# A squared-ReLU MLP as seven block products instead of eight, in a one-core decoder layer

## The chip, the cores and the metric

The kernel runs on one core of one Trainium2 chip. The metric is the device time of one execution in microseconds (us). A core has TensorE (PE, matrix products into PSUM banks), VectorE (DVE), ScalarE (ACT), GpSimd (POOL) and SyncE (SP). Each of them works through its own queue of instructions in order, and an instruction that waits holds up all that stand behind it. SyncE's queue, and in the changed kernel GpSimd's too, issues the transfers between DRAM and the on-chip memory, which the 16 DMA engines then carry out.

## What is computed

One layer of a decoder trunk, for 1024 tokens of width 1024, with 16 meta tokens ahead of them. Four mixers (pooling, RWKV-7, RG-LRU, mLSTM) read one input projection, their outputs go through one output projection, and a dense MLP follows:

```
h  = layer_norm(x)                                  # embedding norm
mix = concat(pool(u), rwkv7(p), rglru(q), mlstm(r)) # from h @ w_in
h  = layer_norm(ALPHA * h + mix @ w_out)            # ln1, "h1" below
ff = square(relu(h @ mlp_w1)) @ mlp_w2              # 1024 -> 4096 -> 1024
h  = layer_norm(ALPHA * h + ff)                     # ln2, the output
```

Both MLP products are a 1024 x 1024 x 4096 product in float32. The change is in these two.

## The kernel before

Every product of float32 operands is made of three matmuls in a faster float type: each operand is split into a high part (a cast on ScalarE, L120 for weights and L125 for the rest) and a low part (the rest, a subtraction on VectorE, L121 and L126), and high x high, high x low and low x high are summed in PSUM. A product of a 128x128 weight tile with 512 tokens is thus three matmuls of 128x512.

The tokens are in eight tiles of 128, and the mixers work on four blocks of two tiles. `PLAN` is a string of steps that sets the order in which the program is written: `S` input projections, `P`, `I`, `C` the three parts of RWKV (projections and products, the triangular inverse by elimination, the chunk recurrence), `M` mLSTM, `L` RG-LRU, `O` pooling, `W` the output projection with its layer norm, each with its block's number. A scheduler then places the instructions on the engines. The mixers are chains of small operations in which TensorE often has nothing to do, so MLP work of the first 512 tokens is put between them: the steps `F0` to `F6` are seven of the MLP's 16 chunks of 256 hidden units, each 48 matmuls of the first product (`mlp_up`, L1162 to L1164), the activation (ScalarE's relu L1167, VectorE's square L1168) and 48 of the second (`mlp_down`, L1186 to L1188), which adds to an accumulator of its token tile (L1191, L1193). `T` (`mlp_in`) loads the h1 tiles again from DRAM (L1139) and transposes them (L178) into the operand.

Some places matter below. The elimination `I` of block b writes its products to DRAM (`dr<-p`, L693), reads them back (`c<-dr`, L695), runs some 60 small steps on VectorE (L752, L753), and goes through DRAM twice more before the matmuls of L719. The last RWKV step of a block ends in L858; its output goes to DRAM and back (`yd<-ys` L563, `x<-yd` L1104) and is split into the operand `mixh`, `mixl` of the output projection (L1125 to L1127, matmuls of 128x256). The result gets its layer norm (L145, L146, L132, POOL's L133, L164, L169) and is stored as `h1d` (L1113).

When the mixers are done, the "late stage" begins: chunk 7 of the first 512 tokens, then `mlp_in` for the second 512, chunks 8 to 15 for all, and chunks 0 to 7 for the second. The last chunk of a tile is followed by its layer norm (L145, L160, L161) and the store of the output (L162). In all the MLP has 3072 matmuls: 672 between the mixers, 2400 in the late stage.

Of the kernel before, what the change touches and what calls it, by code (L numbers as in the profile page):

```python
# [16 lines left out]
P = 128  # L17
# [14 lines left out]
NC = DFF // 256  # L32
# [11 lines left out]
STEPS = PLAN.split()  # L44
EARLY = sum(t[0] == "F" and t.endswith(".2") for t in STEPS)
# [45 lines left out]
class Trunk:  # L91
# [22 lines left out]
    def load_w(self, src, pool=False):  # L114
        nc = self.nc
        raw = self.wsp.tile([P, 1024], F32, name="wraw", bufs=self.wsb[0])
        nc.sync.dma_start(raw, src)
# [149 lines left out]
    def run(self):  # L267
        tc, nc, a = self.tc, self.nc, self.a
        with ExitStack() as top:
# [5 lines left out]
            self.h1d = [self.drp.tile([P, D], F32, name="h1d%d" % t, bufs=1) for t in range(NT)]  # L275
            self.program(top)

    def program(self, top):
# [9 lines left out]
        self.psp = {"b": psum(top, "psB")}  # L288
# [28 lines left out]
        self.h1t, self.acc = [None] * 2, [None] * NT  # L317
        nf = 0
        for st in STEPS:
# [4 lines left out]
            elif k == "R":  # L324
                R.close()
                self.accp = [pool(M, "acc0", "right", 4), None]
                self.h1p = [pool(M, "h1T0", "right"), None]
                self.mdp, self.mdb = pool(M2, "midA", "right"), 1
            elif k == "T":
                self.mlp_in(0)  # L330
            elif k == "F":
# [801 lines left out]
    def mlp_in(self, g, tag="b"):  # L1133

        self.h1t[g] = [self.h1p[g].tile([P, 8, 512], F32R, name="h1T%s" % x) for x in "hl"]
        for i in range(4):
            t = 4 * g + i
            self.acc[t] = self.accp[g].tile([P, D], F32, name="acc")
            self.nc.sync.dma_start(self.acc[t], self.h1d[t])  # L1139
            self.to_feature(self.acc[t], P, *self.h1t[g], i * P, tag)  # L1140
        self.cnt = getattr(self, "cnt", [0, 0])
# [107 lines left out]
```

## Time and profile before

| | before |
|---|---|
| runs (us) | 1373.75, 1377.15, 1373.67 |
| median | 1373.75 |
| profiled execution | 1368.71 |
| its span, first to last instruction | 1366.9 |
| mean granted TensorE clock | 0.983 |
| moved by DMA | 132.54 MB |

The profile is of the execution that took 1368.71 us; times in it count from the start of its span. A row of the timeline has the start in us, the time in us, the engine, the line, the operation, the tile written and the tiles read, and how many were joined in the row; brackets hold the idle time before it and what ended that. "SPq" is SyncE's queue issuing a transfer, so its time is that of the issue, and the landing comes later. A row of the windows has the stretch, its length, the busy time of PE, PE's weight loads, DVE, ACT and POOL with the number of instructions, the granted clock, the share of the DMA engines and GB/s. A row of the page on DMA ends with the size of one transfer and the median time from issue to landing. The slices cut the span into 40 parts of 34.2 us.

### The profile page before, as it was taken

The numbers are of one execution on the slowest core, as the hardware profiler recorded it, in microseconds if no ns is written. First come the engines' busy times: TensorE is split into PE (matmuls) and PEld (weight loads), VectorE is DVE, ScalarE is ACT, GpSimd is POOL, SyncE is SP. The second block draws the span as 40 slices with busy tenths as digits, with TensorE's granted clock in tenths as the row PEclk, the third lists the DMA queues.
The fourth block names the chain that finished last, engine by engine and source line by source line (L and its number), as shares of the span: only waits on it lengthen the run. The fifth ranks groups of instructions, "written<-read, shape, count | busy, mean of one in ns | idle before, by whom it ended". The sixth has DMA issues, their size and how long they took to land.

```text
span 1366.9 us, 20292 instructions
## 1 busy us (share of the span) xinstructions
PE 1313.2 (96%) x8001; PEld 1110.2 (81%) x8001; DVE 843.2 (62%) x1998; ACT 478.4 (35%) x812; POOL 78.9 (6%) x101
## 2 busy tenths in 40 slices
PE   4999999999999999999999999999999999999997
PEld 3989888988999967777688887888888888788886
DVE  8846657865747668476866875454444544844547
ACT  5435474532376342433332423111211112122320
POOL 3110010000100000010001100000000000100001
PEclk9999999997999999999999999999999999999999
DMA  7422204331443432222323951110111011313311
GB/s 246 173 76 78 74 24 137 104 116 51 136 140 131 166 104 71 70 74 82 112 63 123 321 185 63 47 47 31 62 47 47 31 62 58 112 61 109 123 62 62
DMA packets 60128, 132.54 MB, mean 97 GB/s; under 512 B 22752, under 2 KB 29552, under 8 KB 60032
## 3 DMA queue, kind: packets, MB, share of 16 engines
q1 hardware_dynamic: 60032, 131.23, 29.1%
q8 instruction: 63, 1.03, 0.3%
q14 instruction: 33, 0.27, 0.1%
HBM read 113.38 MB, written 17.83 MB: 96 GB/s over the span
## 4 chain that ended last, share of the span: by engine, by line
PE 50%; DVE 4%; POOL 1%; issue 1%; ACT 1%; DMA 0%; DVEq 0%; ACTq 0%; SPq 0%; POOLq 0%
PE c L1162 7%; PE c L1163 7%; PE c L1164 7%; PE c L1186 6%; PE c L1187 6%; PE c L1188 6%; PE b L1186 1%; PE b L1188 1%; PE b L1187 1%; PE b L1164 1%; PE b L1162 1%; PE b L1126 1%; DVE wlo L121 1%; PE b L1127 1%; PE b L1125 1%; PE b L1163 1%
## 5 line engine op out<-in xcount | busy, mean ns | idle before, releaser
L120 ACT CAST whi<-wraw 128x1024 fp32r<-128x1024 f32 x170 | 176.1, 1048 | 457.7 <-PE c L1188 204.8
L121 DVE TENSOR_TENSOR wlo<-wraw,whi 128x1024 fp32r<-128x1024 f32 x170 | 206.0, 1221 | 160.1 <-ACT whi L120 158.1
L450 PE MATMUL b<-hTh,wlo 128*128 128x256 f32 (+1 forms) x672 | 194.6, 290 | 1.6 <-DVE wlo L121 1.6
L449 PE MATMUL b<-hTl,whi 128*128 128x256 f32 (+1 forms) x672 | 195.6, 291 | 0.5 <-DVE hTl L126 0.3
L448 PE MATMUL b<-hTh,whi 128*128 128x256 f32 (+1 forms) x672 | 195.2, 291 | 0.2 <-ACT hTh L125 0.2
L1193 DVE TENSOR_TENSOR acc<-acc,c 128x512 f32<-128x512 f32 x160 | 108.2, 684 | 93.1 <-PE c L1188 93.0
L1186 PE MATMUL c<-whi,midh 128*128 128x512 f32 x400 | 157.5, 394 | 3.0 <-DVE acc L1193 2.9
L1187 PE MATMUL c<-wlo,midh 128*128 128x512 f32 x400 | 157.3, 393 | 0.0
L1162 PE MATMUL c<-h1Th,whi 128*128 128x512 f32 x400 | 156.8, 392 | 0.0
L1163 PE MATMUL c<-h1Tl,whi 128*128 128x512 f32 x400 | 156.7, 392 | 0.0
L1164 PE MATMUL c<-h1Th,wlo 128*128 128x512 f32 x400 | 156.5, 391 | 0.0
L1188 PE MATMUL c<-whi,midl 128*128 128x512 f32 x400 | 155.3, 390 | 0.0
L449 PEld LDWEIGHTS b<-hTl,whi 128*128 128x128 f32 x672 | 129.2, 192 | 3.3 <-issue 1.2
L450 PEld LDWEIGHTS b<-hTh,wlo 128*128 128x128 f32 x672 | 129.0, 192 | 3.2 <-DVE wlo L121 2.1
L448 PEld LDWEIGHTS b<-hTh,whi 128*128 128x128 f32 x672 | 129.2, 192 | 1.5 <-ACT hTh L125 0.7
L1186 PEld LDWEIGHTS c<-whi,midh 128*128 128x128 f32 x400 | 75.1, 188 | 22.6 <-DVE acc L1193 3.8
L1162 PEld LDWEIGHTS c<-h1Th,whi 128*128 128x128 f32 x400 | 75.1, 188 | 17.1 <-DVE acc L1193 0.4
L1188 PEld LDWEIGHTS c<-whi,midl 128*128 128x128 f32 x400 | 75.1, 188 | 16.9 <-DVE midl L126 0.5
L1164 PEld LDWEIGHTS c<-h1Th,wlo 128*128 128x128 f32 x400 | 75.1, 188 | 16.5
L1163 PEld LDWEIGHTS c<-h1Tl,whi 128*128 128x128 f32 x400 | 75.1, 188 | 16.4
L1187 PEld LDWEIGHTS c<-wlo,midh 128*128 128x128 f32 x400 | 75.3, 188 | 15.3
L1168 DVE TENSOR_TENSOR mid_r<-mid_r 128x512 f32<-128x512 f32 x64 | 43.9, 686 | 53.8 <-ACT mid_r L1167 53.8
(358 smaller groups left out, 2236.5 us busy)
## 6 DMA issues: line engine op xcount, KB each, us to landing
wraw<-in_w SPq DMA_DIRECT2D x96, 512.0 KB, 3.5
wraw<-in_w_in SPq DMA_DIRECT2D x42, 512.0 KB, 3.3
wraw<-in_w_out SPq DMA_DIRECT2D x32, 512.0 KB, 3.4
x<-in_x SPq DMA_DIRECT2D x8, 512.0 KB, 4.0
h0d<-x SPq DMA_DIRECT2D x8, 512.0 KB, 3.0
x<-yd SPq DMA_DIRECT2D x8, 512.0 KB, 4.8
x<-h0d SPq DMA_DIRECT2D x8, 512.0 KB, 6.3
h1d<-x SPq DMA_DIRECT2D x8, 512.0 KB, 3.0
```

What stands on the lines that cost most here:

```text
L120: nc.scalar.copy(hi, raw)
L121: (nc.gpsimd if pool else nc.vector).tensor_tensor(lo, raw, hi.bitcast(F32), op=ALU.subtract)
L448: nc.tensor.matmul(pt, lhsT=wh[:, ks], rhs=hh[:, kt, 0:nb], start=(kt == 0), stop=False)
L449: nc.tensor.matmul(pt, lhsT=wh[:, ks], rhs=hl[:, kt, 0:nb], start=False, stop=False)
L450: nc.tensor.matmul(pt, lhsT=wl[:, ks], rhs=hh[:, kt, 0:nb], start=False, stop=(kt == 7))
L1162: nc.tensor.matmul(pt, lhsT=wh[:, ks], rhs=hh[:, kt], start=(kt == 0), stop=False)
L1163: nc.tensor.matmul(pt, lhsT=wh[:, ks], rhs=hl[:, kt], start=False, stop=False)
L1164: nc.tensor.matmul(pt, lhsT=wl[:, ks], rhs=hh[:, kt], start=False, stop=(kt == 7))
L1186: nc.tensor.matmul(pt, lhsT=xh, rhs=wh, start=((c, u) == cu[0]), stop=False)
L1187: nc.tensor.matmul(pt, lhsT=xh, rhs=wl, start=False, stop=False)
L1188: nc.tensor.matmul(pt, lhsT=xl, rhs=wh, start=False, stop=((c, u) == cu[-1]))
L1193: nc.vector.tensor_tensor(acc, acc, pt, op=ALU.add)
```

## The change

Both products are cut into 2x2 blocks and computed with seven block products and some sums of blocks, in Winograd's form of Strassen's scheme, instead of eight: 7 x 192 matmuls of 128x512 for each of the two, 2688 in all. The parts are:

- `mlp_first` (steps `G0` to `G15`, in the place of the `F` steps): 24 matmuls each on the first 512 tokens, 384 in all. After half of them the bank is copied out (`p1`) and stored in DRAM; the whole gives the activation `m11`, also stored in DRAM.
- `w2_sums` (steps `Z0` to `Z3`): four sums of blocks of the second weight, made in DRAM a quarter at a time. SyncE copies a block of 1 MB, an accumulating DMA of GpSimd adds another, for four sums; the third sum starts from the first and the fourth from the third.
- `mlp_sums`, at the start of the late stage: the second 512 tokens of h1 are loaded, transposed (32 transposes, L1207) and combined with the first 512; five operands come out, split into high and low (44 operations on VectorE).
- `mlp_set`, 16 times: the other five products of the first MLP product for 128 rows of each half of the hidden units, 60 matmuls, with the sums of the weight blocks before and the sums of the products, activations and sums of activations behind; two loads of 512 KB, two of 256 KB and six stores of 256 KB.
- `down_product`, seven times 192 matmuls, for the second MLP product: both operands come from DRAM and are split, in groups of 24 matmuls. "11" stands ahead of the sets, "21" behind them; `mlp_out` has the other five, the sums into the accumulators and the layer norms.

The diff, cut to what the text speaks of:

```
-        "M0.1 M0.2 I1 e2 M0.3 Slp1.0 ... O3 R T P2 I2 M2.0 F0.0 C2.0 C2.1 "
-        "F0.1 F0.2 F1.0 F1.1 F1.2 F2.0 F2.1 F2.2 M2.1 F3.0 P3 F3.1 F3.2 I3 M2.2 F4.0 F4.1 C3.0 ...
+        "M0.1 M0.2 I1 e2 Z0 M0.3 Slp1.0 ... W1.0 Z1 Sml1.6 ... O3 R T P2 I2 M2.0 G0 C2.0 C2.1 "
+        "G1 G2 G3 Z2 G4 G5 M2.1 G6 P3 G7 G8 I3 M2.2 G9 C3.0 G10 M3.0 G11 M3.1 G12 W2.0 Z3 M3.2 W2.1 C3.1 "
+        "W2.2 W2.3 W2.4 G13 W2.5 G14 W3.0 W3.1 W3.2 G15 W3.3 W3.4 W3.5")
...
-        self.mlp_chunk([EARLY], [0], "c")
-        self.mlp_in(1, "c")
-        for c in range(EARLY + 1, NC):
-            self.mlp_chunk([c], [0, 1], "c")
-        for c in range(0, EARLY + 1, 2):
-            self.mlp_chunk([k for k in (c, c + 1) if k <= EARLY], [1], "c")
+        self.mlp_sums()
+        self.down_product("11", 0, self.bank[4:8], True)
+        for i in range(4):
+            nc.scalar.copy(self.p1s[i], self.bank[4 + i])
...
+        for k in range(NS):
+            self.mlp_set(k)
+        self.down_product("21", 5, self.bank[4:8], True)
...
+        self.mlp_out(pool(DD, "acc", "right"))
...
+    def w2_sums(self, j):
...
+        jobs = ((1, q(0, 0), q(0, 1)), (3, q(0, 1), q(1, 1)), (2, r[1], q(1, 1)), (4, r[2], q(1, 0)))
+        last = self.last_dma
+        for i, first, more in jobs:
+            with self.tc.issue_after(last):
+                nc.sync.dma_start(r[i], first)
+            nc.gpsimd.dma_start(r[i], more, accum_op=ALU.add)
...
+            tt(v(t1), v(b[0]), h(bh, 0), op=ALU.subtract)
+            tt(v(t1), v(t1), h(bl, 0), op=ALU.subtract)
+            tt(t2, b[1], t1, op=ALU.subtract)
+            tt(t3, b[0], b[1], op=ALU.subtract)
+            tt(v(t4), h(bh, 1), v(t2), op=ALU.subtract)
+            tt(v(t4), v(t4), h(bl, 1), op=ALU.add)
+            for q, z in ((1, t2), (0, t1), (2, t3), (4, b[1]), (3, t4)):
+                self.half_split(tmp, "t", self.tops[q][0][:, :, cs], self.tops[q][1][:, :, cs], v(z), neg=(q == 4))
...
+            tt(acc[t][:, lo], acc[t][:, lo], X[i], op=ALU.add)
+            self.layer_norm(acc[t], P, g2, b2, out=a["out"][t * P:(t + 1) * P], cut=2 if i == 3 else 1)
```

Three places show how the scheduler lays out the change.

SyncE's queue, where the operand of the first 512 tokens is loaded (`h1d_71` to `h1d_74` are the first four tiles of h1, `yd` a mixer's output on its way through DRAM, `dr` and `c` the elimination's). Before:

```order
L1113 DMA h1d_74<-x 128x1024
L117 DMA wraw<-in_w 128x1024 x3
L1139 DMA acc<-h1d_71 128x1024
L1139 DMA acc<-h1d_72 128x1024
L1091 DMA yd_173<-sc_5631 128x2x256
L1139 DMA acc<-h1d_73 128x1024
L1139 DMA acc<-h1d_74 128x1024
L117 DMA wraw<-in_w 128x1024
L693 DMA dr<-p_5817 32x8x32 x4
```

After, with the sums of step `Z2` (`rd_2_209`, `_217`, `_213` and `_221` are its four sums):

```order
L1115 DMA h1d_74<-x 128x1024
L117 DMA wraw<-in_w 128x1024 x4
L1093 DMA yd_317<-sc_5791 128x2x256
L1180 DMA rd_2_209<-in_w 512x512
L1180 DMA rd_2_217<-in_w 512x512
L1144 DMA h1x<-h1d_71 128x1024
L1144 DMA h1x<-h1d_72 128x1024
L1180 DMA rd_2_213<-rd_2_209 16x16384
L1144 DMA h1x<-h1d_73 128x1024
L1144 DMA h1x<-h1d_74 128x1024
L695 DMA dr<-p_5974 32x8x32 x4
L1180 DMA rd_2_221<-rd_2_213 16x16384
```

The first two copies now stand ahead of the first reload, and the third, which waits for GpSimd's addition to `rd_2_209`, ahead of the reload of the second pair of tiles; the fourth stands between the elimination's `dr<-p` and `c<-dr`.

TensorE's queue at the end of the last block's RWKV step, where the output projection of that block follows (`b` is a PSUM bank, `r` the bank of the RWKV step). Before:

```order
L1125 MATMUL b<-whi,mixh 128x256
L856 MATMUL r<-cst,rw_yn 128x128
L858 MATMUL r<-rw_l,lrk 128x128 x2
L1126 MATMUL b<-wlo,mixh 128x256
L1127 MATMUL b<-whi,mixl 128x256
```

After:

```order
L1149 MATMUL b<-h1Tl,whi 128x512
L1149 MATMUL b<-h1Th,wlo 128x512
L858 MATMUL r<-cst,rw_yn 128x128 x2
L860 MATMUL r<-rw_l,lrk 128x128 x2
L1127 MATMUL b<-whi,mixh 128x256
L1128 MATMUL b<-wlo,mixh 128x256
```

Before, the matmuls behind L858 are 92 of the output projection of the block before, then 48 of the MLP; after, all of the block before stand further up, and the 96 behind L860 are those of the last block itself.

VectorE's queue behind the last output projection (`x<-x,b` takes its last bank, the rows behind it are the last layer norm). Before:

```order
L1130 SCALAR_TENSOR_TENSOR x<-x,b 128x256
L169 SCALAR_TENSOR_TENSOR x<-x,ln_rs,bc_b 128x1024
L145 BN_STATS ln_st<-x 128x6
L1168 TENSOR_TENSOR mid_r<-mid_r 128x512
L146 BN_AGGR ln_mv<-ln_st 128x2
L132 TENSOR_SCALAR ln_rs<-ln_mv 128x1
L164 SCALAR_TENSOR_TENSOR x<-x,ln_mv,bc_g 128x1024
L126 TENSOR_TENSOR midl<-mid_r,midh 128x512
```

After (`b_` are the transposed tiles, `tt_` the sums, `t0l` to `t4l` the low parts of the five operands):

```order
L1132 SCALAR_TENSOR_TENSOR x<-x,b 128x256
L169 SCALAR_TENSOR_TENSOR x<-x,ln_rs,bc_b 128x1024
L145 BN_STATS ln_st<-x 128x6
L1213 TENSOR_TENSOR tt_8606<-b_8598,h1Th 128x512
L146 BN_AGGR ln_mv<-ln_st 128x2
L1216 TENSOR_TENSOR tt_8608<-b_8598,b_8604 128x512
L132 TENSOR_SCALAR ln_rs<-ln_mv 128x1
L164 SCALAR_TENSOR_TENSOR x<-x,ln_mv,bc_g 128x1024
L1214 TENSOR_TENSOR tt_8606<-tt_8606,h1Tl 128x512
L169 SCALAR_TENSOR_TENSOR x<-x,ln_rs,bc_b 128x1024
L1215 TENSOR_TENSOR tt_8607<-b_8604,tt_8606 128x512
L126 TENSOR_TENSOR t0l<-tt_8606,t0h 128x4x128
```

Before, the rows between those of the norm are work on MLP chunk 7; after, they are the sums of the second 512 tokens, and 38 more of these follow before the first split of "11".

More of the change, by code (lines that the diff above doesn't have):

```diff
@@ L31 @@
 BIG = 2.0 ** 100
-NC = DFF // 256
+NS = DFF // 256
 PLAN = ("e0 Srw0.0 Srw0.1 k Srw0.2 Srw0.3 Srw0.4 Srw0.5 Srw0.6 Slp0.0 P0 I0 C0.0 Slp0.1 C0.1 Slp0.2 C0.2 "
         "Slp0.3 Slp0.4 Slp0.5 L0 Sml0.0 O0 Sml0.1 O1 Sml0.2 P1 Sml0.3 L1 Sml0.4 Sml0.5 Sml0.6 Sml0.7 M0.0 "
[5 rows of a table removed]
[5 rows of a table added]
 STEPS = PLAN.split()
-EARLY = sum(t[0] == "F" and t.endswith(".2") for t in STEPS)
 BLOCKS = [[0, 1], [2, 3], [4, 5], [6, 7]]
@@ L275, in run @@
             self.h1d = [self.drp.tile([P, D], F32, name="h1d%d" % t, bufs=1) for t in range(NT)]
+            dt = lambda n: [self.drp.tile([P, 512], F32, name="%s_%d" % (n, k), bufs=1) for k in range(NS)]
+            self.p1d = dt("p1d")
+            self.md = {q: dt("md" + q) for q in ("11", "21", "22", "n1", "s2", "s3", "s4")}
+            self.rd = {q: [self.drp.tile([4 * P, 512], F32, name="rd%d_%d" % (q, j), bufs=1) for j in range(4)] for q in (1, 2, 3, 4)}
             self.program(top)
@@ L316, in program @@
         M, M2 = ExitStack(), ExitStack()
-        self.h1t, self.acc = [None] * 2, [None] * NT
-        nf = 0
         for st in STEPS:
@@ L1130, in w_out, with mlp_in @@
             nc.vector.scalar_tensor_tensor(hs, hs, ALPHA, pt, op0=ALU.mult, op1=ALU.add)
-    def mlp_in(self, g, tag="b"):
-        self.h1t[g] = [self.h1p[g].tile([P, 8, 512], F32R, name="h1T%s" % x) for x in "hl"]
+    def mlp_in(self):
+        self.h1t = [self.h1p.tile([P, 8, 512], F32R, name="h1T" + x) for x in "hl"]
         for i in range(4):
[L1137 to L1141, printed above, removed]
@@ new lines, in mlp_in, with mm3, mlp_first @@
+            x = self.mdp.tile([P, D], F32, name="h1x")
+            self.nc.sync.dma_start(x, self.h1d[i])
+            self.to_feature(x, P, *self.h1t, i * P, "b")
+    def mm3(self, pt, wh, wl, hh, hl, start, stop):
+        mm = lambda *p, **k: self.nc.tensor.matmul(*p, skip_group_check=True, **k)
+        mm(pt, lhsT=wh, rhs=hh, start=start, stop=False)
+        mm(pt, lhsT=wh, rhs=hl, start=False, stop=False)
+        mm(pt, lhsT=wl, rhs=hh, start=False, stop=stop)
+    def mlp_first(self, k):
+        nc = self.nc
+        wh, wl = self.load_w(self.a["w1"][k])
+        pt = self.ps("b", [P, 512])
+        for kt in range(8):
+            ks = slice(kt * P, (kt + 1) * P)
+            self.mm3(pt, wh[:, ks], wl[:, ks], self.h1t[0][:, kt], self.h1t[1][:, kt], kt == 0, kt % 4 == 3)
+            if kt == 3:
+                p1 = self.mdp.tile([P, 512], F32, name="p1")
+                nc.scalar.copy(p1, pt)
+                nc.sync.dma_start(self.p1d[k], p1)
+        m = self.mdp.tile([P, 512], F32, name="m11")
+        nc.scalar.activation(m, pt, AF.Relu)
+        nc.vector.tensor_tensor(m, m, m, op=ALU.mult)
+        nc.sync.dma_start(self.md["11"][k], m)
@@ new lines, in down_product @@
+    def down_product(self, q, w, banks, start, group=2):
+        nc, w2 = self.nc, self.a["w2"]
+        for g in range(0, NS, group):
+            ops = []
+            for k in range(g, g + group):
+                raw = self.wcp.tile([P, 1024], F32, name="raw", bufs=4)
+                nc.sync.dma_start(raw[:, 0:512], self.md[q][k])
+                if w in (0, 5, 6):
+                    f, d = {0: (0, 0), 5: (1, 0), 6: (1, 1)}[w]
+                    src = w2[16 * f + k][:, 512 * d:512 * d + 512]
+                else:
+                    src = self.rd[w][k // 4][(k % 4) * P:(k % 4 + 1) * P]
+                nc.sync.dma_start(raw[:, 512:1024], src)
+                ops.append((self.pair(raw[:, 0:512]), self.pair(raw[:, 512:1024])))
+            for i, pt in enumerate(banks):
+                ts = slice(i * P, (i + 1) * P)
+                for j, (a, b) in enumerate(ops):
+                    self.mm3(pt, a[0][:, ts], a[1][:, ts], b[0], b[1], start and g + j == 0, g + j == NS - 1)
```

227 lines of the change are left out of this document (152 added, 75 removed), and 8 rows, old and new, of the table PLAN.

## The prediction

> **What bounds the kernel now.** I read the page first (busy shares, slices, chain), then the stages in windows, then the places that the change touches in the timeline.
>
> ```profile
> PE 1313.2 (96%) x8001; PEld 1110.2 (81%) x8001; DVE 843.2 (62%) x1998; ACT 478.4 (35%) x812; POOL 78.9 (6%) x101
> GB/s 246 173 76 78 74 24 137 104 116 51 136 140 131 166 104 71 70 74 82 112 63 123 321 185 63 47 47 31 62 47 47 31 62 58 112 61 109 123 62 62
> PE 50%; DVE 4%; POOL 1%; issue 1%; ACT 1%; DMA 0%; DVEq 0%; ACTq 0%; SPq 0%; POOLq 0%
> ```
>
> TensorE is busy in 96% of the span, and half of the chain that ended last is TensorE. But a busy TensorE is not one at full pace, so I take the windows.
>
> ```profile
> 440.00:470.00 30.00, 30.00 (x256) 30.00 (x255) 19.70 (x46) 11.13 (x17) 2.99 (x2) 1.00 0.45 158
> ...
> 490.00:741.00 251.00, 242.28 (x1534) 186.98 (x1533) 173.54 (x557) 83.95 (x166) 15.53 (x21) 0.99 0.25 78
> ...
> 828.00:1359.00 531.00, 527.99 (x2298) 430.74 (x2297) 266.93 (x359) 115.87 (x155) 10.20 (x7) 1.00 0.19 62
> 900.00:1000.00 100.00, 100.00 (x437) 81.81 (x436) 47.57 (x65) 17.54 (x24) 0.00 (x0) 1.00 0.13 43
> ```
>
> From 828 to 1359 us there is only MLP work. Its pace is 437 matmuls of 128x512 in 100 us, 0.2288 us each; VectorE is busy for half of the stage and DMA for a fifth. That stage is bound by the number of matmuls. From 490 to 741 us the mixers of the last token blocks run, with MLP matmuls put between; there the mixers' own chains share the bound, and VectorE is busy for 173.5 of 251 us. Matmuls of 128x256 have a pace of 30/256 = 0.117 us.
>
> **The term that is removed.** 3072 MLP matmuls become 2688; the shape and the three passes per product stay. 384 x 0.2288 = **-87.9 us**. By place: the mixer stage holds 672 of them now and will hold 384 (-65.9 us), the late stage 2400 and then 2304 (-22.0 us). Everything below is what is paid back.
>
> **The seam behind the last output projection.** Now the late stage begins like this:
>
> ```profile
> 805.64 0.41 DVE L1130 SCALAR_TENSOR_TENSOR x<-x,b 128x256 f32<-128x256 f32 x1
> ...
> 810.67 1.28 DVE L169 SCALAR_TENSOR_TENSOR x<-x,ln_rs,bc_b 128x1024 f32<-128x1024 f32 x1
> 820.92 2.35 PE L178 MATMUL c<-cst,acc 128*128 128x128 f32 x20
> 824.74 1.85 PE L178 MATMUL c<-cst,acc 128*128 128x128 f32 x12 [1.47 <-DVE h1Tl L126]
> 824.00 4.87 DVE L126 TENSOR_TENSOR h1Tl<-c,h1Th 128x512 fp32r<-128x512 f32 x8
> ```
>
> Between the last layer norm (810.67) and the transposes (820.92) TensorE has a whole MLP chunk to do, and the eight splits of 0.61 us (4.87/8) cost it an idle of about 1.9 us (5.7 us for 32 transposes that take 3.8 at the pace of the first 20). In the new order nothing of the MLP can come before the sums: TensorE's row after the last W_out matmul is the 32 transposes, then the products of m11, whose second pass needs the split `wl`, and on VectorE that split stands behind 43 of the 44 sums and splits of the second 512 tokens, which begin in among the last layer norm. The rest of that norm takes about 6.5 us of VectorE (two rows of 0.41 and 1.28 above, and their like for the other tile), 43 x 0.61 = 26.2, the split itself 0.6: 33 us from the last W_out matmul to the first full MLP product. TensorE has 3.8 us of transposes in it, and 1.9 were idle before: **+27**. ScalarE's and the reload's work of the last tile lies beside it. Ends: +20 if a third of the sums runs ahead, +31 if the last tile's way through DRAM comes late.
>
> **The entry of the last block's output projection.**
>
> ```profile
> 740.49 0.71 PE L858 MATMUL r<-rw_l,lrk 64*128 64x128 f32 x4
> 742.91 0.41 DVE L862 TENSOR_TENSOR ys<-ys,r 128x256 f32<-128x256 f32 x1
> 743.35 0.38 SPq L563 DMA_DIRECT2D yd<-ys  x1
> 746.56 0.39 SPq L1104 DMA_DIRECT2D x<-yd  x1
> 752.23 1.05 ACT L125 CAST mixh<-x 128x1024 fp32r<-128x1024 f32 x1 [1.68 <-PE b L1126]
> ```
>
> From the last RWKV matmul (741.2) over two DMAs to the cast operand (753.3) it is 12 us. Now 92 matmuls of the block before and 48 of the MLP fill that. In the new order the block's 96 matmuls stand directly behind the RWKV matmuls: **+12** (ends +9, +14).
>
> **The clock.** Each of these two new idles may bring half speed for a while, as here:
>
> ```profile
> 226.00:228.00 2.00, 2.00 (x12) 1.96 (x10) 1.13 (x5) 0.36 (x1) 0.00 (x0) 0.50 0.98 356
> ```
>
> At half clock 2 us hold 1 us of work. Taking 3.4 us at half clock after each idle gives 2 x 1.7 = **+3.4** (0 to 7). The Trainium skill, "TensorE: Matmul & The Clock Gate", Part 1, says that an idle window of about 3.4 us halves the clock and that about 3.4 us of sustained work restore it; the row shows the half clock, though after small gaps. By the rule the sum would be the same, and it speaks against a change that opens such gaps.
>
> **The end of the kernel.**
>
> ```profile
> 1359.07 0.40 PE L1188 MATMUL c<-whi,midl 128*128 128x512 f32 x1
> 1359.51 0.69 DVE L1193 TENSOR_TENSOR acc<-acc,c 128x512 f32<-128x512 f32 x1
> 1360.23 0.69 DVE L145 BATCH_NORM_STATS2 ln_st<-acc 128x6 f32<-128x512 f32 x1
> 1362.59 1.41 DVE L161 SCALAR_TENSOR_TENSOR acc<-acc,ln_rs,bc_ln2b 128x512 f32<-128x512 f32 x2
> ```
>
> One token tile is left behind the last matmul: 1359.5 to 1364.0. In the new order all four tiles of the second half get their last sum from the last product, whose banks close 1.4 us apart. One tile costs VectorE 4.5 to 5.2 us (the rows above, and one more L145 of 0.69), four 18 to 21, beginning 3.7 us ahead of the end: VectorE ends 14.5 to 17 us behind the last matmul instead of 4.9. **+10** (ends +9, +12).
>
> **The sums of W2 in DRAM.** Four times (Z0 to Z3) SyncE's queue issues a copy of 1 MB, GpSimd adds 1 MB to it by an accumulating DMA, SyncE waits for that and copies the result, GpSimd adds again, and SyncE waits again for its last copy. Behind each wait stand the mixers' loads and stores. No DRAM-to-DRAM copy and no accumulating DMA is in the trace. Nearest rows:
>
> ```profile
> wraw<-in_w SPq DMA_DIRECT2D x96, 512.0 KB, 3.5
> yd<-sc SPq DMA_DIRECT2D x8, 256.0 KB, 3.5
> acc<-h1d SPq DMA_DIRECT2D x8, 512.0 KB, 5.5
> out<-acc SPq DMA_DIRECT2D x2, 256.0 KB, 2.0
> ```
>
> With 321 GB/s from the slices, a second 512 KB adds 1.6 us to 3.5: a copy is 5.1 us. An addition reads two megabytes: 1.9 + 2 x 3.3 = 8.4 us. Its ends are 3.5 (as one load) and 15 (the 5.5 us row for each half MB, with another trip). So one link is 13.5 us and a Z holds SyncE's queue 27 us. Who stands behind:
>
> ```profile
> 183.81 0.35 SPq L117 DMA_DIRECT2D wraw<-in_w_in  x1
> 206.18 3.62 SPq L117 DMA_DIRECT2D wraw<-in_w_in  x2
> 377.15 0.43 SPq L1108 DMA_DIRECT2D x<-h0d  x1
> 387.40 0.33 SPq L117 DMA_DIRECT2D wraw<-in_w_out  x1
> 479.22 0.37 SPq L1091 DMA_DIRECT2D yd<-sc  x1
> 479.63 0.97 SPq L1139 DMA_DIRECT2D acc<-h1d  x2
> 480.34 1.07 PE L178 MATMUL b<-cst,acc 128*128 128x128 f32 x8
> 489.69 0.47 PE L1162 MATMUL b<-h1Th,whi 128*128 128x512 f32 x1
> 500.23 1.80 SPq L693 DMA_DIRECT2D dr<-p  x4
> 552.87 0.69 PE L719 MATMUL r<-ys,p 32*32 32x32 f32 x32
> 635.32 1.81 SPq L693 DMA_DIRECT2D dr<-p  x4
> 693.64 0.69 PE L719 MATMUL r<-ys,p 32*32 32x32 f32 x32
> ```
>
> - Z0 starts behind the load of 183.8 and lets go at 211; the loads of 206.2 come 5 us late, mostly ahead of need: +1. Z1 starts near 377.6 and lets go at 404.6, W_out loads from 387.4 on stand behind it, the buffers are ahead of TensorE: +3.
> - Z2 stands between `yd<-sc` (479.2) and the reload of h1 for the MLP's operand. The first pair of tiles waits behind 2 MB of copies, the second pair for the first addition: issued at 493, landed at 502, last transpose at 505 where the first MLP matmul was at 489.7. Some small matmuls go ahead meanwhile: +13.
> - Z3 holds `dr<-p` of the last elimination (now at 635.3, right behind its products). By the new order Z3 starts 12 us before those products, so the wait is about 15 us. From `dr<-p` to L719 it is 52.6 us (500.2 to 552.9) and 58.3 now, with MLP work of VectorE in between; with less of that I take 40. TensorE has 66 MLP matmuls (15.1), 173 of W_out (20.2) and some 8 us of small ones to do in that time, 43. 15 + 40 + 1 - 43 = +13.
>
> Together **+30**. With additions of 3.5 us it is 11, with 15 us 62. The loads and stores of the late stage I cost at nothing: a set of 60 matmuls (13.7 us) covers VectorE's 15 operations of 0.61 (9.2) and 3.1 MB (229 GB/s against 321 seen); without that cover see the third rival.
>
> **The sum.** -87.9 + 27 + 12 + 3.4 + 10 + 30 = -5.5 us. The profiled execution took 1368.71 us (span 1366.9 us), which gives 1363.2; the median of the runs, 1373.75, is 5.04 above it, so I forecast **1368 us**. A measurement can tell about 0.3%, 4.1 us, from no change. Additions between 5.5 and 11 us and the seam's ends make the forecast's own range 1357 to 1380.
>
> **Rivals.**
> - The DRAM sums are cheap or hidden: additions of 3.5 us, Z's 11 instead of 30, so 1349 us; wholly hidden 1338. For it: DMA has a share of only 0.25 from 490 to 741. Against: Z2's place has no slack at all (479.63 to 480.34).
> - Slower, by one mechanism: the accumulating DMAs are slow, and SyncE's queue stands at Z2 and Z3. It decides from 39 us in sum on, additions of about 10.5 us. With 15 us (Z0 3, Z1 12, Z2 20, Z3 27) it is 62 - 30 = +32: 1400 us.
> - The late stage becomes bound by DMA. A set's ten transfers, one after the other, would take 4 x 3.5 + 6 x 2.0 = 26 us against 13.7: 16 x 12.3 = +197, 1565 us. Against it, slice 22 moved 321 GB/s with loads of 512 KB of 3.5 us each, so they overlap. The Trainium skill, "DMA: Bandwidth & Descriptors", Bandwidth, asks for transfers of at least 1 MiB for three quarters of peak. By its fit (2.0 us and bytes at 436 GB/s) a set would take an estimated 27 us if nothing overlapped.
> - The mixers' chains, not matmuls, set the pace from 490 to 741: the elimination keeps its 52.6 us (+12.6), and with 60 instead of 81 matmuls between the second-last block's RWKV steps (21 x 0.229 = 4.8) and as much again for the last block nothing is won there: +22, 1390 us. For it: VectorE's 173.5 of 251. Against: MLP work on VectorE shrinks too.
>
> **How the numbers follow.** Forecast 0.42, sums hidden 0.25, slow additions 0.20, DMA bound 0.03, chains 0.10. Of the forecast's own cases about half (0.22) lie more than 4.1 us below 1373.75, 0.14 within it and 0.06 above. Faster 0.25 + 0.22 = 0.47, same 0.14, slower 0.06 + 0.20 + 0.03 + 0.10 = 0.39. The range of 8 in 10 runs from 1341, near the hidden sums, to 1402, just over the slow additions.
>
> **What would show it.** Right: an idle of TensorE of about 27 us behind the last W_out matmul with VectorE's L1213 to L1218 as releaser; 12 us before the last block's W_out; four layer norms behind the last matmul; the wait of transposes for `h1x` near 480 us; 0.229 us per matmul in the sets. Wrong: SyncE's second copies of a Z more than 10 us or less than 5 behind the first's landing; TensorE waiting for `raw` or splits in the sets; a last elimination much later or earlier against its products.

## The result, and the profile after

The changed kernel takes **1396.46 us** in the median of four runs (1390.15 to 1398.34), beside 1373.8 for the kernel before: a ratio of 1.0151, with a 95% interval of 1.0114 to 1.0188. The forecast was 1368 us, so the change costs 23 us where 5.5 were to be won. The time lies inside the stated range, on the other side of no change. The execution profiled took 1390.15 us (span 1388.1), 21.4 us more than the one profiled before. Ratios here and below are of fast executions alone; left out are two of 2.98 and 6.59 ms in one experiment, whose cause is open, and the one of 1389.89 us that the trace of the copies from SyncE is of.

The page of the changed kernel: spans, TensorE, the granted clock by slices, GB/s by slices, and the new queue of GpSimd's transfers.

```profile
span 1388.1 us, 21003 instructions
PE 1249.0 (90%) x7619; PEld 1065.3 (77%) x7619; DVE 868.5 (63%) x2122; ACT 616.7 (44%) x1128; POOL 91.7 (7%) x117
PEclk9999997899997977997889787999999999999998
GB/s 249 164 81 74 73 170 195 96 144 62 137 253 188 137 201 224 183 69 202 240 137 108 131 191 174 187 222 243 226 229 235 197 304 250 195 187 200 192 220 114
q0 software_dynamic: 8448, 16.78, 7.3%
```

TensorE is busy for 64 us less than before and the span is 21 us longer: TensorE stands idle. The mean granted clock is 0.931 (0.983 before), and in the slices the clock is down in the mixer stage and at the seam, not behind it. Windows show where (columns as before):

```profile
188.00:293.50 105.50, 95.29 (x646) 85.34 (x644) 68.36 (x240) 50.78 (x100) 11.35 (x18) 0.84 0.59 155
355.30:500.00 144.70, 128.48 (x1016) 124.01 (x1015) 79.01 (x165) 67.35 (x101) 11.97 (x15) 0.93 0.62 184
500.00:582.00 82.00, 64.39 (x300) 48.27 (x299) 45.10 (x147) 29.71 (x60) 6.87 (x7) 0.81 0.81 215
628.00:728.00 100.00, 83.55 (x453) 65.24 (x453) 57.89 (x219) 30.93 (x64) 9.85 (x16) 0.80 0.75 199
814.00:853.00 39.00, 14.16 (x52) 10.21 (x51) 37.54 (x62) 20.75 (x37) 2.99 (x2) 0.61 0.41 140
900.00:1000.00 100.00, 100.00 (x443) 82.84 (x442) 68.93 (x108) 62.39 (x111) 0.00 (x0) 1.00 0.68 231
```

The first four hold Z0 to Z3: idle time on TensorE of 10 to 18 us in each, with a DMA share of 0.6 to 0.8 and a clock of 0.80 to 0.93. The fifth is the seam, and the sixth shows the sets running at TensorE's pace with 231 GB/s beside. What TensorE waited for, by the longest single waits behind one of 13.4 us at the kernel's start, which the kernel before has too (us in total, times, longest):

```profile
PE l L1049 <- ACT lr_x L1050: 11.1, 1, 11.1
PE b L1127 <- ACT mixh L125: 9.6, 1, 9.6
PE b L178 <- DMA h1x<-h1d: 9.4, 1, 9.4
PE bank L1223 <- ACT t0h L125: 8.7, 1, 8.7
```

The second, third and fourth are three places of the prediction: the last block's output projection, the transposes behind Z2, and the seam. The first, in the stretch behind Z1, was not foreseen.

Since the mixers' own instructions are the same in all kernels, the same matmul can be looked up in each trace. This table has the time at which it is reached, from the timelines; the last two kernels are experiments told below.

| reached (us) | before | changed | no sums | sums of an eighth |
|---|---|---|---|---|
| end of block 0's RWKV step, ahead of Z0 | 188.4 | 187.9 | 189.7 | 188.3 |
| second elimination's matmuls | 278.4 | 293.5 | 281.1 | 278.3 |
| end of block 1's RWKV step | 350.3 | 355.3 | 354.4 | 350.2 |
| last input projection (Z1 before it) | 475.7 | 499.9 | 480.0 | 475.8 |
| third elimination's matmuls (Z2) | 552.9 | 581.9 | 549.8 | 544.6 |
| end of block 2's RWKV step | 597.3 | 628.1 | 596.0 | 590.4 |
| fourth elimination's matmuls (Z3) | 693.6 | 727.8 | 681.5 | 674.0 |
| end of block 3's RWKV step | 740.9 | 771.3 | 720.6 | 717.2 |
| last W_out matmul | 803.8 | 813.6 | 762.6 | 758.2 |
| last matmul | 1359.1 | 1371.4 | 1319.9 | 1315.3 |
| span | 1366.9 | 1388.1 | 1336.5 | 1332.0 |

At the end of block 3's RWKV step the changed kernel is 30 us late, though it has left out MLP matmuls all the way. It makes good 20 us to the last W_out matmul, where the kernel before still does MLP work. The late stage takes 557.8 us instead of 555.2, and the end behind the last matmul 16.7 instead of 7.8.

### The profile page after: what moved, and what is told of

Its sections match the earlier page's. It is cut to its first block, busy times and chain, and to the rows that moved or that the text cites. A ratio compares the mean times of both kernels' runs of the same rounds, so it can differ in the third digit from the quotient of the medians.

```text
span 1388.1 us, 21003 instructions
## 1 busy us (share of the span) xinstructions
PE 1249.0 (90%) x7619; PEld 1065.3 (77%) x7619; DVE 868.5 (63%) x2122; ACT 616.7 (44%) x1128; POOL 91.7 (7%) x117
## 5 line engine op out<-in xcount | busy, mean ns | idle before, releaser
L126 DVE TENSOR_TENSOR wl<-raw,wh 128x512 fp32r<-128x512 f32 x240 | 151.5, 685 | 121.3 <-ACT wh L125 121.2
L125 ACT CAST wh<-raw 128x512 fp32r<-128x512 f32 x240 | 133.5, 618 | 196.0 <-PE bank L1149 189.7
L1149 PE MATMUL bank<-wl,wh 128*128 128x512 f32 x448 | 175.4, 392 | 4.2 <-DVE wl L126 4.2
L1149 PE MATMUL bank<-wh 128*128 128x512 f32 x448 | 175.3, 393 | 1.1 <-ACT wh L125 1.1
L1149 PE MATMUL bank<-wh,wl 128*128 128x512 f32 x448 | 175.2, 391 | 0.0
L121 DVE TENSOR_TENSOR wlo<-wraw,whi 128x1024 fp32r<-128x1024 f32 x90 | 109.7, 1220 | 102.6 <-ACT whi L120 101.1
L120 ACT CAST whi<-wraw 128x1024 fp32r<-128x1024 f32 x90 | 94.3, 1047 | 146.4 <-PE b L451 42.6
L1149 PEld LDWEIGHTS bank<-wl,wh 128*128 128x128 f32 x448 | 84.7, 189 | 22.7 <-DVE wl L126 5.2
L1149 PEld LDWEIGHTS bank<-wh 128*128 128x128 f32 x448 | 84.8, 190 | 19.2 <-ACT wh L125 1.5
L1149 PEld LDWEIGHTS bank<-wh,wl 128*128 128x128 f32 x448 | 84.7, 189 | 17.4
L1127 PEld LDWEIGHTS b<-whi,mixh 128*128 128x128 f32 x256 | 51.6, 202 | 13.3 <-ACT mixh L125 9.9
## 6 DMA issues: line engine op xcount, KB each, us to landing
rd<-in_w POOLq DMA_DIRECT2D x16, 1024.0 KB, 10.9
```

What stands on the lines that cost most here:

```text
L120: nc.scalar.copy(hi, raw)
L121: (nc.gpsimd if pool else nc.vector).tensor_tensor(lo, raw, hi.bitcast(F32), op=ALU.subtract)
L125: self.nc.scalar.copy(hi, src)
L126: self.nc.vector.tensor_tensor(lo, src, hi.bitcast(F32), op=ALU.subtract)
L1127: nc.tensor.matmul(pt, lhsT=xh, rhs=wh, start=(kt == 0), stop=False)
L1149: mm = lambda *p, **k: self.nc.tensor.matmul(*p, skip_group_check=True, **k)
```

## The experiments

Ratios are to the kernel before in the same job (medians of 1369 to 1372 us there), with their 95% intervals.

**Without the sums.** `w2_sums` isn't called, and the operands that were sums are read from one block of W2:

```
-                self.w2_sums(b)
+                pass
-                    src = self.rd[w][k // 4][(k % 4) * P:(k % 4 + 1) * P]
+                    src = w2[16 + k][:, 0:512]
```

> The changed kernel without any of the sums of W2 in DRAM: neither copies nor additions are issued, and the second product's operands that were sums are read from one block of W2 instead (so the result leaves the sums out; loads, splits and matmuls of the late stage stay as many and as large). Theory A, SyncE's queue standing behind the additions opens gaps at Z0 to Z3 and each gap brings half clock: the changed kernel's 1396 us falls by 35 to 50, to 1346 to 1361 us, and the stretches at half clock near 228, 412, 504 and 692 us are gone. Theory B, the mixers' chains have too little other work around them whatever the sums do: a fall of under 15 us, 1381 us or more, and the half-clock stretches from 500 to 730 us stay.

Measured: 1336.52 us, ratio 0.976 (0.973 to 0.979). The sums cost 3.9% of the time, some 54 us; in the traces 51.6. The idle of 9.4 us ahead of the transposes and the 11.1 us of L1049 are gone from TensorE's list. Of the stretches at half clock that theory A named, those near 412 and 692 us are gone; near 228 us 3.4 us stay, and ahead of 504 us 17 (486.4 to 503.5). By the table, Z1 costs 19 us (144.6 against 125.6 us from block 1's RWKV step to the last input projection), Z2 12, Z3 14, and 4 more come behind Z3. Z0 costs 14, but then 11 come back: the stretch behind it holds the same matmuls and takes 56 us in the changed kernel and 66 in the one before, where the clock is down (changed, then before):

```profile
300.00:356.00 56.00, 55.67 (x452) 49.36 (x450) 38.31 (x141) 20.83 (x40) 3.12 (x4) 1.00 0.26 81
```

```profile
285.00:351.00 66.00, 65.78 (x450) 58.28 (x448) 38.45 (x141) 20.73 (x40) 3.12 (x4) 0.82 0.22 74
```

**The sums without SyncE's waits**: all four copies from blocks of W2, seven additions.

```
+        for i, first in ((1, q(0, 0)), (3, q(0, 1)), (2, q(0, 0)), (4, q(0, 0))):
...
+        for i, more in ((1, q(0, 1)), (3, q(1, 1)), (2, q(0, 1)), (4, q(0, 1)), (2, q(1, 1)), (4, q(1, 1)), (4, q(1, 0))):
+            nc.gpsimd.dma_start(r[i], more, accum_op=ALU.add)
```

> The same sums, but the third and fourth are built from blocks of W2 alone: SyncE issues four copies that wait for nothing, GpSimd makes seven additions of 1 MB instead of four. Theory A, what costs is that SyncE's queue waits: nearly all of what the kernel without sums wins comes here too, 1350 to 1370 us, though 28 instead of 16 MB are added. Theory C, what costs is the traffic of the sums, or GpSimd's own queue, behind whose waiting additions the layer norms' and the RWKV step's powers stand: no gain, 1390 us or more, with TensorE waiting for rows of GpSimd.

Measured: 1434.56 us, ratio 1.0477 (1.0416 to 1.0538), the slowest of all. Theory A as it stood, SyncE's queue alone, falls. TensorE's longest waits are now for a row of GpSimd, which stands behind the additions:

```profile
PE r L632 <- POOL rw_rn L133: 35.7, 7, 19.0
```

**The sums in place, all on GpSimd** (the copies too):

```
-                nc.sync.dma_start(r[i], first)
+                nc.gpsimd.dma_start(r[i], first)
```

> The sums stay between the mixers where they are, but GpSimd issues the copies as well, so SyncE's queue never waits for them. Theory A2, GpSimd's queue is as costly a place as SyncE's, since the powers of the RWKV step and the layer norms stand behind: not better than the changed kernel by more than 15 us, ratio to before 1.005 to 1.03, with TensorE waiting for rows of GpSimd. Theory A, only SyncE's queue matters: ratio 0.975 to 0.99.

Measured: 1416.26 us, ratio 1.0325 (1.0284 to 1.0367), with 27.1 us of waits for that row of GpSimd. Its queue is the worse place: the same bytes cost some 24 us more than with SyncE sharing them. But in both runs the waits stay, only in another queue (and the first adds 28 MB instead of 16), so two more runs took waits and bytes apart.

**All the waits, an eighth of the bytes.** SyncE's rows around Z0 to Z3 stand as in the changed kernel, but each transfer moves 128 KB:

```
-        q = lambda f, d: w2[16 * f + 4 * j:16 * f + 4 * j + 4, :, 512 * d:512 * d + 512].rearrange("n p c -> (n p) c")
+        q = lambda f, d: w2[16 * f + 4 * j][0:64, 512 * d:512 * d + 512]
```

> The changed kernel's queues at Z0 to Z3 as they are, row for row: the same copies, additions and waits, but each over an eighth of the rows (128 KB), into tiles that nothing reads; the second product reads single blocks of W2, so the result leaves the sums out. Theory A2, what stands behind waiting rows pays for the number of waits: two thirds or more of the 50 us stay, ratio to before 1.000 or more. Theory C, the bytes are what is paid for, as transfer time that is waited for: most goes, ratio 0.976 to 0.987, with a link of 4 to 6 us in place of 17.

Measured: 1337.34 us, ratio 0.9765 (0.9732 to 0.9798), the same as without sums. Here is SyncE's queue at Z0, first in the changed kernel:

```profile
183.64 1.25 SPq L1180 DMA_DIRECT2D rd<-in_w  x2
189.74 0.37 SPq L565 DMA_DIRECT2D yd<-ys  x1
201.65 17.09 SPq L1180 DMA_DIRECT2D rd<-rd  x2
218.83 1.01 SPq L117 DMA_DIRECT2D wraw<-in_w_in  x2
```

and with an eighth of the bytes:

```profile
184.03 1.21 SPq L1180 DMA_DIRECT2D rs<-in_w  x2
190.16 0.37 SPq L565 DMA_DIRECT2D yd<-ys  x1
191.26 10.62 SPq L1180 DMA_DIRECT2D rs<-rs  x2
206.01 3.64 SPq L117 DMA_DIRECT2D wraw<-in_w_in  x2
```

The last row of each is the load that the waits hold up: 218.8 against 206.0, and 206.2 in the kernel before. A link still takes 7 and 10 us (184.0, 191.3, 201.4), not the 4 to 6 expected, but SyncE is through before it is needed. The same waits at the same places cost nothing when the transfers behind them are short.

**All the bytes, no waits.** First from GpSimd, eight copies of 1 MB per Z step that nothing reads:

```
+            for i, (f, d) in enumerate(((0, 0), (0, 1), (0, 1), (1, 1), (0, 0), (1, 1), (1, 0), (1, 0))):
+                t = self.drp.tile([4 * P, 512], F32, name="tr%d_%d" % (i, j), bufs=1)
+                nc.gpsimd.dma_start(t, q(f, d))
```

> The kernel without sums (the second product reads single blocks of W2, so the result leaves the sums out), but at each Z step GpSimd issues eight independent copies of 1 MB from DRAM to DRAM, 32 MB in all as in the changed kernel; nothing waits for them and nothing reads them. Theory A2, the cost of the sums is what stands behind waiting transfers in the queues: within 12 us of the kernel without sums, ratio to before 0.974 to 0.985. Theory C, the traffic itself delays the mixers' loads and stores: half or more of the 50 us come back, ratio 0.994 or more.

Measured: 1383.14 us, ratio 1.0114 (1.0075 to 1.0153). GpSimd reached these steps at other times (near 53, 371, 611 and 696 us). By the same landmarks the first cost nothing, the second 17 us, the last two 27. The window behind the second burst, and the same without sums:

```profile
380.00:400.00 20.00, 9.53 (x70) 9.33 (x69) 2.75 (x3) 2.82 (x5) 0.00 (x0) 0.77 1.02 341
```

```profile
380.00:400.00 20.00, 19.95 (x163) 19.54 (x162) 5.68 (x6) 13.77 (x21) 0.00 (x0) 1.00 0.41 146
```

With the DMA engines full (share 1.02, 341 GB/s), TensorE does 70 matmuls where it did 163. Then from SyncE, at the places of Z0 to Z3:

> The bytes at the same places without a wait: at each Z step SyncE issues eight independent copies of 1 MB (the result leaves the sums out; nothing waits for them and nothing reads them). Theory C, the transfers themselves stand ahead of the mixers' loads on the DMA engines: 35 us or more over the kernel without sums, ratio 1.000 or more. Theory A2, the waits are what costs: under 15 us, ratio 0.976 to 0.987. By the copies of the GpSimd variant, 8 MB take some 21 to 25 us of the DMA engines.

Measured: ratio 1.0033 (1.0007 to 1.006), 2.7 points above the kernel without sums, 37 us. No row waits for one of these copies, and yet SyncE comes past them late:

```profile
399.42 21.00 SPq L1179 DMA_DIRECT2D tr<-in_w  x8
420.51 3.38 SPq L117 DMA_DIRECT2D wraw<-in_w_in  x1
```

Issuing the eight copies of Z1 takes SyncE 21 us, where a pair takes 1.25. So theory C holds in the main: bytes that nobody waits for bring back 37 of the 54 us, whether the engines are full or the queue doesn't take more. What the other 17 are, the waits or the additions themselves, these runs do not part, and the quarter of the sums below shows that waits are not free either.

**The sums in the late stage**, all on GpSimd, behind the sets 0, 3, 6 and 9:

> The changed kernel with the sums of W2 moved out of the mixers: the same copies and additions, all issued by GpSimd, begin behind the sets 0, 3, 6 and 9 of the late stage, where GpSimd has nothing else to do and SyncE waits for none of them. Theory A2, the cost is what stands behind the waiting transfers in SyncE's and GpSimd's queues between the mixers: nearly all that the kernel without sums wins, a ratio to before of 0.97 to 0.985 (1328 to 1352 us beside a before of 1370 to 1373). Theory C, the traffic of 32 MB itself costs wherever it stands: the sets, which have a DMA share of 0.66 already, slow down, TensorE waits for raw tiles, and the ratio stays above 0.99.

Measured: 1385.35 us, ratio 1.0095 (1.0064 to 1.0125). The mixers are as without sums (last W_out matmul at 760.7 us), but the late stage takes 606.7 us instead of 557.3. So theory A2's forecast fell here. Part of it was this kernel's own: GpSimd held the activation tile with which the sums were kept back until a set was done, so that ScalarE, and TensorE behind it, waited for up to 13.8 us.

**The order at the seam.** First the whole product of m11 ahead of the token sums, then half of it:

```
-        self.mlp_sums()
-        self.down_product("11", 0, self.bank[4:8], True)
+        self.down_product("11", 0, self.bank[4:8], True)
+        self.mlp_sums()
```

> The changed kernel with the product of m11 (192 matmuls, 44 us) written ahead of the sums of the second 512 tokens, which it does not need; everything is computed. Theory A, TensorE waits at the seam for VectorE's sums because the split of the product's operand stands behind them: 25 to 32 us less, 1364 to 1371 us. Theory D, the wait is for the last tile's way through DRAM or for the banks, not for the order on VectorE: under 10 us.

Measured: 1392.55 us, ratio 1.017 (1.0126 to 1.0213): no gain that can be told. TensorE's rows show why:

```profile
829.97 1.22 PE L1149 MATMUL bank<-wh 128*128 128x512 f32 x2 [4.31 <-ACT wh L125]
...
875.90 1.03 PE L1207 MATMUL bank<-cst,h1x 128*128 128x128 f32 x8
879.80 0.73 PE L1223 MATMUL bank<-t0h,identr 128*128 128x512 f32 x2 [2.87 <-ACT t0h L125]
887.11 0.79 PE L1149 MATMUL bank<-t0h,wh 128*128 128x512 f32 x1 [6.58 <-ACT wh L125]
```

The product gets going 16 us behind the last W_out matmul (814.2) instead of 34, but the last tile's eight transposes now stand behind all 192 matmuls, and its sums open a second gap.

> The changed kernel with half of the product of m11 written ahead of the sums of the second 512 tokens and half behind, so that neither the first matmuls nor the last tile's transposes stand behind everything else. With the whole product ahead, TensorE's first gap shrank by about 18 us, but a second one of about 11 us opened ahead of the sets. Theory A, the seam is a matter of order on VectorE and TensorE: both gaps shrink, 12 to 20 us less than the changed kernel, ratio to before 1.000 to 1.008. Theory D, the last tile's way through DRAM and the splits bound the seam in any order: under 6 us, ratio 1.012 or more.

Measured: 1377.14 us, ratio 1.0038 (1.0015 to 1.0061), 1.1 points less than the changed kernel. The late stage takes 541.9 us instead of 557.8: the second gap is gone. So 16 us of the seam were a matter of order. A first gap of 16 us stays, in which TensorE's longest waits are for the last tile's reload (5.8) and a cast of ScalarE (4.3).

**Both together**, the late sums as they were and then with a mark of its own instead of the held tile:

```
-            self.last_pool = nc.gpsimd.tensor_tensor(mark, m22[:, 0:1], self.eps, op=ALU.add).ins
+            nc.scalar.copy(mark, m22[:, 0:1])
+            self.last_pool = nc.gpsimd.tensor_tensor(mark, mark, self.eps, op=ALU.add).ins
```

> Both together: the sums on GpSimd in the late stage and the product of m11 in two halves. If the two costs are separate, the gains add: ratio to before 0.96 to 0.975 (1316 to 1338 us), faster than both kernels. If the late stage has no room for the sums, above 0.985.

> The sums on GpSimd in the late stage and the split product, as before, but the mark that holds the sums back until a set is done is now a small tile of its own and no longer the activation tile, which kept ScalarE and with it TensorE waiting for GpSimd. If the late sums' cost of 49 us was mostly that hold: ratio to before 0.97 to 0.983. Theory C, the DMA engines are full there (a share of 1.06 from 900 to 1000 us): ratio 0.99 or more, with TensorE's waits in the sets still there.

Measured: 1370.73 us, ratio 0.9993 (0.9968 to 1.0018), and 1359.42 us, ratio 0.9917 (0.989 to 0.9945). The gains do not add: 0.96 to 0.975 was expected of the first, 0.97 to 0.983 of the second. The hold was a part, but the late stage still takes 579.6 us, 38 more than with the split alone:

```profile
850.00:900.00 50.00, 49.04 (x216) 39.92 (x215) 33.32 (x53) 28.23 (x52) 4.50 (x7) 1.00 1.07 325
900.00:950.00 50.00, 42.69 (x175) 34.23 (x174) 27.18 (x44) 24.50 (x45) 4.12 (x5) 0.93 1.09 347
```

The sets need 231 GB/s, and with the sums the engines are full (a share of 1.07 and 1.09) at 325 to 347: 16 MB of copies and 16 of additions cost there too.

**A quarter of the sums at the start** of the mixers, three quarters behind the sets 1, 5 and 9:

> The fastest kernel so far (sums on GpSimd in the late stage, product of m11 in two halves; ratio 0.992), with a quarter of the sums put at the start of the mixers, near 53 us, where 8 MB of copies delayed nothing, and three quarters behind the sets 1, 5 and 9. If bytes cost where the DMA engines or the loads behind are needed, and nothing elsewhere: a quarter of the late sums' 38 us goes, ratio 0.983 to 0.988. If GpSimd's waits at the start hold up the mixers: 0.992 or more.

Measured: 1352.21 us, ratio 0.987 (0.9819 to 0.9921), the fastest that computes everything, though its interval overlaps that of the kernel just above, and the traces differ by only 1.4 us. The late stage falls by 20 us to 559.3, but the early quarter costs 17 us at the end of block 0's RWKV step (207.2 against 190). The ratio lies where the first case had it, and yet the second case's mechanism is what the trace shows: eight transfers of 1 MB at the same place cost nothing as copies that nobody waits for, but here GpSimd's additions wait for copies, and its row of a layer norm stands behind them (at 73.58 us, with the copies alone at 58.21):

```profile
73.58 0.59 POOL L133 TENSOR_TENSOR ln_rs<-ln_rs,mhalf 128x1 f32<-128x1 f32 x1
74.22 1.28 DVE L169 SCALAR_TENSOR_TENSOR x<-x,ln_rs,bc_b 128x1024 f32<-128x1024 f32 x1 [13.37 <-POOL ln_rs L133]
```

VectorE waits 13.4 us for that row. So a wait costs too, where something needed stands behind it.

**The sums on the chip** instead of in DRAM, from blocks loaded for the last five products:

```
+                if w == 4:
+                    nc.gpsimd.tensor_tensor(ra, ra, rb, op=ALU.add)
...
+                    tt(x1, x0, x1, op=ALU.add)
```

> Everything is computed, without sums in DRAM: in the last five products each operand of W2 is added up on the chip (VectorE, and GpSimd for half of the four-block sum) from the blocks themselves, which are loaded for it; the product of m11 stands in two halves around the sums of the tokens. The mixers should be as in the kernel without sums (50 us less than the changed kernel), the seam as with the split product (16 less), and the last five products somewhat slower (20 us more, since the four-block sum loads 1.25 MB per 128 rows and 2.75 us): ratio to before 0.973 to 0.987, faster than both kernels. If the loads of the last five products bind harder, above 0.99.

Measured: 1365.85 us, ratio 0.9968 (0.9949 to 0.9986). That is 0.3% below the kernel before, where 1.3 to 2.7% were expected. The mixers are as without sums, but the last products pay 42 us instead of 20, and not for the loads that were suspected: TensorE waits there for splits (13.6 us on VectorE's, 13.1 on ScalarE's).

**The clock at the last block's entry.** On that kernel, 72 matmuls whose result nothing reads ("idle" ones) in the wait:

> The kernel with the sums on the chip, and 72 idle matmuls of 128x256 (8.4 us, nothing reads their bank) between the last RWKV step and the last block's output projection, where TensorE otherwise waits about 10 us. If half clock after an idle is what the wait brings on top, the 13.7 us at half clock behind it go and the stretch from the last RWKV matmul to the last W_out matmul shortens from 42 to 36 to 39 us. If the clock does not follow TensorE's work, it stays at 42 or grows.

Measured: ratio 0.9979 (0.9965 to 0.9994), and the stretch takes 43.6 us instead of 42.0. The windows, without the idle matmuls and with them:

```profile
720.00:731.00 11.00, 0.91 (x6) 0.71 (x5) 2.50 (x6) 1.43 (x2) 0.00 (x0) 0.56 0.65 222
731.00:762.00 31.00, 30.49 (x213) 28.56 (x212) 15.29 (x20) 9.10 (x10) 0.00 (x0) 0.94 0.47 154
```

```profile
726.00:744.00 18.00, 17.52 (x127) 17.52 (x128) 4.43 (x5) 4.05 (x5) 0.00 (x0) 0.83 0.50 166
744.00:771.00 27.00, 24.07 (x172) 21.96 (x171) 14.51 (x20) 7.10 (x9) 1.53 (x1) 1.00 0.51 155
```

The clock does follow TensorE's work (0.94 becomes 1.00 for the projection), but the idle matmuls themselves begin at half clock and run into the projection's time. The expectation of 36 to 39 us fell: nothing is won.

**The kernel before with less between the mixers**:

```
+                        if tag == "c":
                             nc.tensor.matmul(pt, lhsT=wh[:, ks], rhs=hl[:, kt], start=False, stop=False)
```

> The kernel before, with the second of the three matmuls of every MLP product left out where it stands between the mixers (224 of 672 matmuls of 128x512, so the first 512 tokens' first chunks lack a term); every load, split, sum and wait stays. If matmuls bound that stage: 224 x 0.2288 = 51 us less, 1323 us. Theory B, the mixers' chains bound it once filler is taken away: 25 us or less, 1349 us or more, with more idle and half clock on TensorE between 490 and 741 us.

Measured: 1347.11 us, ratio 0.9833 (0.9798 to 0.9868): 23 us for 51 us of matmuls. Theory B holds. Its window, against 242.28 us busy at clock 0.99 in the kernel before:

```profile
490.00:741.00 251.00, 233.58 (x1479) 177.76 (x1478) 189.20 (x586) 92.39 (x177) 16.97 (x23) 0.94 0.29 91
```

Up to the last W_out matmul TensorE is idle for 56 us instead of 42, and busy at half clock for 77 us instead of 40. Half clock does half the work, so the second is worth an estimated 18 us: what the thinning did not win went to the clock at least as much as to idle.

## Why the prediction was wrong

- **The matmuls removed**, -87.9: right in the late stage, where the pace held (443 recorded in 100 us, 437 before). In the mixer stage it was the wrong unit. Without sums that stage is 41.2 us shorter (762.6 against 803.8), not 65.9. Of the missing 24.7 the entry of the last block's projection, forecast at 12, explains a wait of 10. The other 15 are what the fourth rival (chains, weight 0.10) or half clock can take, and the traces do not part them: without sums TensorE is idle for 57 us up to the last W_out matmul instead of 42, 10 of the difference at the entry, and busy at half clock for 79 us instead of 40, worth up to an estimated 20. That less filler is worth less than its time, the thinned kernel before showed (23 of 51 us).
- **The seam**, +27: right. The late stage is 2.6 us longer with 22.0 us of matmuls less, +24.6 with its clock, and VectorE is busy for all of the stretch from the last W_out matmul to the second pass of the product:

```profile
814.00:848.14 34.14, 9.30 (x41) 6.45 (x39) 33.99 (x57) 20.75 (x37) 2.99 (x2) 0.62 0.37 131
```

  The releasers named on TensorE are not VectorE's sums, as forecast, but mostly ScalarE's casts (13.6 us) and the last tile's reload (5.7). Another order took away 16 of the 24.6.
- **The last block's entry**, +12: right, a wait of 9.6 us and half clock behind it.
- **The end**, +10: right. 16.7 us lie behind the last matmul instead of 7.8:

```profile
1371.44 0.39 PE L1149 MATMUL bank<-wh,wl 128*128 128x512 f32 x1
1383.71 1.41 DVE L161 SCALAR_TENSOR_TENSOR acc<-acc,ln_rs,bc_ln2b 128x512 f32<-128x512 f32 x2
```

- **The sums of W2**, +30: the step that failed. The kind was right, a queue held by transfers, the size was not: 54 us by the ratios, 51.6 by the traces (41 of them more idle on TensorE up to the last W_out matmul, 98 us against 57, and an estimated 11 more at half clock). Both parts of a link were low (a copy 5.1, an addition 8.4):

```profile
rd<-in_w POOLq DMA_DIRECT2D x16, 1024.0 KB, 10.9
rd<-in_w SPq DMA_DIRECT2D x8, 1024.0 KB, 10.0
rd<-rd SPq DMA_DIRECT2D x8, 6.9
```

  A link took 18.0 and 16.7 us at Z0 (183.6, 201.65, 218.3), and SyncE was let go at 218.8 instead of 211. By the prediction's own two points (30 us at a link of 13.5, 62 at 20.1) the eight links, 18 us in the mean, would give about 52, so the total follows from the size of a link. Where it falls does not. Z2 (+12 for 13) and Z3 (+14 for 13) came out in number, in part by luck: at Z2 the third copy left 19.5 us behind the first two (503.8 to 523.3), and at Z3 the elimination's store was held for 10 us instead of 15 (656.2 to 666.5), while its way from there to L719 took 61 us instead of the 40 assumed, as it does without the sums (62). Z1 is the miss: "the buffers are ahead of TensorE" gave it 3, and it took 19. Its first W_out loads, issued from 387.4 us on before, stood behind both waits:

```profile
401.96 0.47 SPq L1180 DMA_DIRECT2D rd<-rd  x1
402.54 0.52 SPq L117 DMA_DIRECT2D wraw<-in_w_out  x1
419.36 0.47 SPq L1180 DMA_DIRECT2D rd<-rd  x1
419.92 1.01 SPq L117 DMA_DIRECT2D wraw<-in_w_out  x2
```

  The buffers do not reach over 15 us and another 17. This lies near the second rival (additions of about 10.5 us and above decide for slower), which had a chance of 0.20 and forecast 1400 us.
- **The clock**, +3.4: too small. Where 3.4 us at half clock were taken after each of two idles, the entry had 17.1 us of it and the seam 30.7. And it was not only those two: each Z brought some as well (0.84, 0.93, 0.81 and 0.80 above; 0.94, 1.00, 0.88 and 0.90 without the sums), and one stretch of the kernel before (0.82) went away. Up to the last W_out matmul TensorE was busy at half clock for 102 us, against 40 in the kernel before: an estimated 31 us of work, which lie inside the parts above and are no further term. The Trainium skill, "TensorE: Matmul & The Clock Gate", Part 1, has half clock after an idle window of about 3.4 us. At the seam the rows agree; in the kernel before its longest stretch at half clock begins with TensorE recorded busy throughout (changed, then before):

```profile
818.50:821.90 3.40, 0.00 (x0) 0.00 (x0) 3.40 (x6) 1.72 (x3) 1.47 (x1) 1.00 0.56 187
821.90:852.60 30.70, 11.63 (x33) 8.21 (x34) 29.80 (x50) 17.23 (x31) 0.00 (x0) 0.50 0.44 147
```

```profile
297.50:300.90 3.40, 3.40 (x26) 3.02 (x25) 1.61 (x6) 0.00 (x0) 0.00 (x0) 1.00 0.14 53
300.90:324.80 23.90, 23.90 (x105) 20.68 (x106) 8.59 (x36) 4.80 (x13) 1.01 (x1) 0.50 0.07 22
```

  So idle alone does not tell when it comes, and what sets its length is open.

With the parts as measured: -87.9 + 24.7 (mixers) + 24.6 + 8.9 + 51.6 = +21.9, against 21.2 between the spans. The parts are differences between the same landmarks, so that they add up proves none of the causes.

The rival in which the late stage is bound by DMA was rightly small: the sets kept TensorE's pace beside 231 GB/s. The Trainium skill, "DMA: Bandwidth & Descriptors", Bandwidth, asks for transfers of at least 1 MiB for three quarters of peak; here 256 and 512 KB sufficed with many under way. What counted for the late sums was that all engines were full, at 325 to 347 GB/s.

## What to carry to other kernels

A saving counted in matmuls holds only where matmuls set the pace: between chains the filler that was thinned gave less than half its time, and part of what it did not give was half clock. Price a transfer that is put between such chains by the time its bytes take on the DMA engines, also where nothing waits for it; the same waits with an eighth of the bytes were free. Then look at what stands behind each wait in the queue that waits: at the start of the mixers the same bytes cost nothing as plain copies and 17 us as additions for which GpSimd's queue stood still. And look for the work behind a seam that needs none of the sums before it, and for the few instructions that must not stand behind it.

## What the runs showed of the hardware

- An accumulating DMA of 1 MB from DRAM to DRAM landed after 10.9 us in the median, a plain copy after 6.9 us (contiguous, issued alone) to 10.0 us (rows of 2 KB, issued in pairs).
- Eight such copies on SyncE's queue took 21 us to issue at Z1 though nothing waited; the queue itself then holds up what stands behind.
- With the engines' share at 1.02 to 1.09, the core moved 325 to 347 GB/s. A full share is no fixed rate: from 504.46 to 521.52 us of the changed kernel it was 287 GB/s at 1.05, from 34.65 to 38.06 of the one before 375 at 1.01.
- After an idle of 3.4 us and more the granted clock stayed at half for 7 to 31 us (197.3, 228.0, 671.7 and 821.9 us of the changed kernel), also with TensorE at work again; and it was half for 24 us in the kernel before with no idle recorded ahead.
